# Differential attention: one ScalarE copy per head output, the sub-norm weight in a later product, and score matmuls of a unit under a scheduler priority

## Chip, cores and metric

The kernel runs on one core of one Trainium2 chip. The metric is device time in microseconds (us) of one execution; several executions are measured and the median is taken. One further execution was recorded by the hardware profiler; all rows of the profile come from it. TensorE is written PE in the profile (PEld is its weight load), VectorE DVE, ScalarE ACT, GpSimd POOL and SyncE SP.

## The reference, cut to what matters

Two layers work on 512 latent tokens and 256 context tokens of width 1024. Layer 0 is differential attention with 8 heads, layer 1 is grouped-query attention. The change lies in layer 0:

```python
def diff(qq, kk, vv, gate):
    o1 = sweep_attention(qq[..., 0, :], kk[..., 0, :], vv)
    o2 = sweep_attention(qq[..., 1, :], kk[..., 1, :], vv)
    o = o1 - lam.astype(o1.dtype) * o2
    o = rms_norm(o, subln_g) * (1.0 - lam_init)
    o = o.reshape(o.shape[0], o.shape[1], BRANCH_WIDTH)
    return (o * jax.nn.silu(gate)) @ w_out
```

Each head has two score maps of 64-wide queries and keys; their softmaxes are subtracted before the product with the values (128 wide). The head output `o` is normalised over its 128 features (`rms_norm`), weighted by `subln_g`, and gated.

## The kernel before

Every matrix product in float32 accuracy is made of three matmuls on a high part and a low part of each operand (`mm3`, lines 142 to 145; `pv_mm`, lines 147 to 150, for the product with the values). High parts are cast on ScalarE, low parts subtracted on DVE or POOL. PSUM is held in four single banks (`bk0` to `bk3`), handed out in turn by `pj` and `trp` and given back by `close`, and in two pairs of banks for scores (`sc0`, `sc1`, handed out by `sc2`).

A planner (`flow`, line 346) writes the program order of layer 0. For each head there are three streams: score units (S), transposes of the probabilities (T) and products with the values (M). Each step has a due time, a cost and lags to earlier steps; between steps the planner inserts pieces of the projections of later heads (`qk_proj`, `v_proj`, `z_proj`), which fill PE. A fourth stream (X) holds the sub-norm of each head (`subln`, line 974; `subln_last`, line 986, for the last head), a fifth the sums for the modulation weights (`grp_mm`, line 728).

The final order on each engine is made by the scheduler of the language. It takes instructions by priority: the place in the program less an offset that a step's `high_priority` gives, once their operands are ready by its own reckoning. The offsets of the streams in layer 0 are in `HOT0` (line 36): 4200 for S, 3100 for T, 0 for M and 4800 for X. Within an engine, instructions then run strictly in that order.

A score unit (`unit`, line 861) covers 128 queries against 768 keys. It issues 12 matmuls of 384 columns: two column halves, three high/low terms, and for each of these one matmul per map. The two maps use 64 rows each, rows 64 to 127 and rows 0 to 63 of the array. `after(prev)` (line 297) makes each come behind the one before it on PE; other matmuls may come between. `unit_ctx` (line 899) does the same for the 256 context queries with 12 matmuls of 256 columns. DVE takes the maximum (line 885), ScalarE the exponential (line 888), POOL and DVE scale and subtract the two maps (lines 893 and 896). PE transposes the result (line 945), ScalarE casts the high part `ah` (line 950), DVE subtracts the low part `al` (line 951), and `pv_mm` multiplies with the values.

A head output of 256 tokens stands in one bank when the last `pv_mm` of a chunk is done (`mstep`, line 954). There are 24 such outputs: 8 heads with 3 chunks. ScalarE squares it out of the bank into the tile `sq` (line 968), DVE multiplies it out of the bank by the sub-norm weight into `gT` (line 969 through the helper `scaled`, so that the profile shows line 221), and the bank is given back. The tile `sq` exists once. `subln` then takes the sum of squares over the 128 features by a matmul with ones (`colsum`, lines 377 to 382: a cast on ScalarE, a subtraction on POOL, two matmuls on PE), forms the inverse root by a logarithm and an exponential on ScalarE (lines 979 and 981), multiplies `gT` by it on DVE (line 982; line 997 for the last head) and by the gate on POOL (line 839).

Of the kernel before, what the change touches and what calls it, by code (L numbers as in the profile page):

```python
# [26 lines left out]
SC_A = 64 ** -0.5  # L27
SC_B = 128 ** -0.5
HOT = 500
HF0 = ((('qk', 1), ('qk', 2), ('z', 0)), (('qk', 3),), (('z', 1), ('v', 2), ('qk', 4), ('z', 2)), (('qk', 5), ('z', 3)), (('v', 4), ('qk', 6), ('z', 4)), (('qk', 7), ('z', 5)), (('v', 6), ('z', 6)), (('z', 7),))  # L30
FILL0 = tuple(f for hf in HF0 for f in hf)
ATT = 15.0
# [49 lines left out]
def tile_backbone(  # L82
# [134 lines left out]
    def scaled(eng, dst, src, s_):  # L217
        if eng == "a":
            nc.scalar.activation(dst, src, AF.Copy, scale=s_)
        else:  # L220
            (nc.vector if eng == "v" else nc.gpsimd).tensor_scalar(dst, src, s_, 1.0, ALU.mult, ALU.mult)  # L221
# [74 lines left out]

    def after(prev):
        return nullcontext() if prev is None else tc.issue_after(prev.ins)

    def hot(f, *args):  # L300
        with tc.high_priority(offset=HOT):
# [415 lines left out]
    with tc.tile_pool(name="t0", bufs=1) as t0:  # L717
# [140 lines left out]
        def s_units(h, qts):  # L858
            res = []

            def unit(qt):
                k0, nk = (0, T) if qt < NQ else (512, C)
                l, ps_ = small(2), []
                if nk == T:
                    sc = [sc2(), sc2()]
                else:
                    if h < KT - 1 or qt == NQ:
                        sts["sc"] = sc2()
                    sc = [sts["sc"]] * 2
                w = 384 if nk == T else 256  # L870
                qh, ql, kh_, kl_ = qk[h]
                tok = slice(qt * P, (qt + 1) * P)
                prev = None
                for j in range(nk // w):
                    c = slice(k0 + j * w, k0 + j * w + w)
                    for i, (a, b) in enumerate(((qh, kh_), (qh, kl_), (ql, kh_))):
                        for m in (1, 0):
                            r = slice(m * 64, m * 64 + 64)
                            with after(prev):
                                prev = nc.tensor.matmul(  # L880
                                    sc[m][:, j if nk == T else m, :w], a[r, tok], b[r, c], start=i == 0, stop=i == 2)
                for m in range(2):
                    scv = sc[m][:, :, :384] if nk == T else sc[m][:, m, :256]
                    mx = small()
                    nc.vector.tensor_reduce(mx, scv, AX.XY if nk == T else AX.X, ALU.max, negate=True)  # L885
                    pt = t0.tile([P, T], F32, tag=f"p{m}", name=nm("p"), bufs=4 if m == 0 else 2)[:, :nk]
                    pv_ = pt.rearrange("p (j n) -> p j n", j=2) if nk == T else pt
                    nc.scalar.activation(pv_, scv, AF.Exp, bias=mx, accum_out=l[:, m:m + 1])  # L888
                    ps_.append(pt)
                    r = l[:, m:m + 1]  # L890
                    nc.vector.reciprocal(r, r)
                    if m == 0:
                        scaled(EP0, pt, pt, r)
                    else:
                        nc.vector.tensor_tensor(r, r, nlam, ALU.mult)
                        nc.vector.scalar_tensor_tensor(ps_[0], pt, r, ps_[0], ALU.mult, ALU.add)  # L896
                        res.append(ps_[0])

            def unit_ctx():
                sc = [sc2(), sc2()]  # L900
                qh, ql, kh_, kl_ = qk[h]
                prev = None
                for qt in (NQ, NQ + 1):
                    tok = slice(qt * P, (qt + 1) * P)
                    for i, (a, b) in enumerate(((qh, kh_), (qh, kl_), (ql, kh_))):
                        for m in (1, 0):
                            r = slice(m * 64, m * 64 + 64)
                            with after(prev):
                                prev = nc.tensor.matmul(
                                    sc[m][:, qt - NQ, :C], a[r, tok], b[r, S:T], start=i == 0, stop=i == 2)  # L910
                l = [small(2), small(2)]
                pts = []
                for m in range(2):
                    mx = small(2)
                    nc.vector.tensor_reduce(mx, sc[m][:, :, :C], AX.X, ALU.max, negate=True)
                    pt = t0.tile([P, T], F32, tag=f"p{m}", name=nm("p"), bufs=4 if m == 0 else 2)
                    pts.append([pt[:, e * C:(e + 1) * C] for e in range(2)])
                    for e in range(2):
                        nc.scalar.activation(pts[m][e], sc[m][:, e, :C], AF.Exp, bias=mx[:, e:e + 1], accum_out=l[m][:, e:e + 1])
                    nc.vector.reciprocal(l[m], l[m])  # L920
                    if m:
                        nc.vector.tensor_tensor(l[m], l[m], nlam.to_broadcast([P, 2]), ALU.mult)
                    for e in range(2):
                        if m == 0:
                            scaled(EP0, pts[0][e], pts[0][e], l[0][:, e:e + 1])
                        else:
                            nc.vector.scalar_tensor_tensor(pts[0][e], pts[1][e], l[1][:, e:e + 1], pts[0][e], ALU.mult, ALU.add)
                res.extend(pts[0])

            if qts[0] == NQ and h < KT - 1:  # L930
                return res, [Step(unit_ctx, 1.0)]
            sts = {}
            cost = 1.2 if qts[0] < NQ else 0.5
            return res, [Step(lambda qt=qt: unit(qt), cost) for qt in qts]

        def pv_steps(h, at, ch, after, ts, ms):
            kts = range(6) if ch < 2 else range(4, 6)
            st = {}

            def tstep(kt):  # L940
                tr = trp()
                for e in range(2):
                    j = kt + e - kts[0]
                    for i, a in enumerate(at):
                        nc.tensor.transpose(tr[:, e * 256 + i * P:e * 256 + (i + 1) * P], a[:, j * P:(j + 1) * P], ident)  # L945
                if h == 0 and ch == 0 and kt == 0:
                    t0.tile([P, 8], F32, name="pad_a")
                ah = t0.tile([P, 512], F32R, tag="ah", name=nm("ah"), bufs=AB)
                al = t0.tile([P, 512], F32R, tag="al", name=nm("al"), bufs=AB)
                nc.scalar.copy(ah, tr)  # L950
                nc.vector.tensor_tensor(al, tr, f32(ah), ALU.subtract)
                st[kt] = ah, al

            def mstep(kt):
                if kt == kts[0]:
                    st["o"] = pj(256)
                o = st["o"]
                ah, al = st[kt]
                vh, vl = vt[h]
                vc = slice((h % 2) * P, (h % 2) * P + P)  # L960
                pv_mm(o, vh, vl, vc, ah, al, kt, kt == kts[0], kt == kts[-2])
                if kt == kts[-2]:
                    if ch == 2:
                        pvdone.add(h)
                    sl = slice(ch * 256, ch * 256 + 256)
                    if ch == 0:
                        ogs[h] = t0.tile([P, T], F32, tag="sq", name=nm("sq"), bufs=1)
                    nc.scalar.activation(ogs[h][:, sl], o, AF.Square)
                    scaled(EG0, gT[h][:, sl], o, subg)
                    close(o)  # L970

            chunk(0, tstep, mstep, kts[::2], [after], ts, ms)

        def subln(h):
            sq, og = ogs[h], gT[h]
            for (a, b) in halves:
                o2 = pj(384)
                colsum(o2, sq[:, a:b], [t0.tile([P, 512], F32R, tag="tmp", name=nm("sqs"), bufs=3)[:, :b - a] for _ in range(2)])
                nc.scalar.activation(sq[:, a:b], o2, AF.Ln, scale=1.0 / P, bias=eps)  # L979
                close(o2)  # L980
            nc.scalar.activation(sq, sq, AF.Exp, scale=-0.5)
            nc.vector.tensor_tensor(og, og, sq, ALU.mult)
            done.add((h, "o"))
            gate_mul(h)

        def subln_last(a, b):
# [7 lines left out]
            nc.scalar.activation(sq, o2, AF.Ln, scale=1.0 / P, bias=eps)  # L994
            close(o2)
            nc.scalar.activation(sq, sq, AF.Exp, scale=-0.5)
            nc.vector.tensor_tensor(og, og, sq, ALU.mult)
            VP[EGL].tensor_tensor(og, og, szt[h][:, a:b], ALU.mult)
            nc.scalar.copy(ghi[h][:, a:b], og)
            nc.vector.tensor_tensor(glo[h][:, a:b], og, f32(ghi[h][:, a:b]), ALU.subtract)  # L1000
# [692 lines left out]
```

## Time and profile before

| What | Value |
|---|---|
| runs | 824.39, 826.21 and 827.17 us; median 826.21 us |
| profiled execution | span 822.0 us from its first to its last instruction; no other time of it is given |
| granted TensorE clock, mean | 0.992 |
| DVE, ACT, POOL busy | 482.3, 457.1, 440.4 us |
| DMA | 77.77 MB, mean 95 GB/s |

The groups of the profile stand by line, engine, operation and tile: `L968 ACT ACTIVATE sq<-bk 128x256` is the square of line 968, read from a bank and written to `sq`. Behind it come the count, the busy time in us with the mean of one in ns, and the idle time of the engine just before such instructions with what ended it. In a row of the list of waits stand the waiting engine and line, what ended the wait, the sum in us, how often, and the longest. In a timeline row the first number is the start in us from the start of the span, the second the duration of the merged group. Ends of matmuls are modelled, so PE work is measured here from start to next start.

Layer 0's attention takes the span from about 81 us to 484 us, where the last head's sub-norm ends; layer 1's attention lies from about 620 us to 782 us.

### The profile page before, as it was taken

The page shows a single profiled execution, that of the slowest core. Times are in us where ns is not written, and L with a number is a line of the kernel's source. Part 1 is how long each engine was busy: PE and PEld are TensorE (multiplying, and loading weights), DVE is VectorE, ACT ScalarE, POOL GpSimd, SP SyncE. Part 2 cuts the span into 40 slices and gives each one's busy share as a digit, 9 for nine tenths or more (in the row PEclk, how much of TensorE's full clock was granted, in tenths as well). Part 3 has the DMA queues.
Part 4 walks back from the last instruction along what each step waited for, and adds up shares of the span by engine and source line. Part 5 has one row for each costly group of instructions (what it writes and reads, how often), then busy time and mean ns, then how long its engine had stood idle before and what let it go on. Part 6 is the DMA issues. An engine that isn't in the chain of part 4 may idle for free. (4 is left out here: it accounts for less than half of the span.)

```text
span 822.0 us, 14412 instructions
## 1 busy us (share of the span) xinstructions
PE 792.7 (96%) x5482; PEld 703.0 (86%) x5482; DVE 482.3 (59%) x896; ACT 457.1 (56%) x1001; POOL 440.4 (54%) x538
## 2 busy tenths in 40 slices
PE   7999999999999999999999999999999999999997
PEld 5678897788887898787988898889999899898986
DVE  3425566754768524675458952579546566755534
ACT  6534357664575544765556852674446576666631
POOL 4544766856367744665822311587788656733101
PEclk9999999999999999999999999999999999999999
DMA  9934211122053321323330045033421210301102
GB/s 300 347 131 142 77 39 52 52 77 90 28 154 98 122 101 65 116 78 118 113 104 26 27 151 182 1 110 103 154 79 52 78 52 1 103 26 52 50 28 103
DMA packets 41540, 77.77 MB, mean 95 GB/s; under 512 B 3584, under 2 KB 18688, under 8 KB 41472
## 3 DMA queue, kind: packets, MB, share of 16 engines
q1 hardware_dynamic: 38048, 71.71, 26.4%
q10 hardware_dynamic: 3424, 5.15, 1.8%
q8 instruction: 43, 0.70, 0.3%
q14 instruction: 25, 0.20, 0.1%
HBM read 70.56 MB, written 2.10 MB: 88 GB/s over the span
## 5 line engine op out<-in xcount | busy, mean ns | idle before, releaser
L207 POOL TENSOR_TENSOR wlo<-raw,whi 128x256 fp32r<-128x256 f32 x200 | 152.0, 792 | 72.8 <-ACT whi L213 63.1
L143 PE MATMUL bk<-whi,h 128*128 128x256 f32 (+1 forms) x592 | 176.9, 302 | 1.1 <-ACT p L1459 0.8
L144 PE MATMUL bk<-wlo,h 128*128 128x256 f32 (+1 forms) x592 | 176.2, 299 | 0.2 <-DVE wlo L207 0.2
L145 PE MATMUL bk<-whi,h 128*128 128x256 f32 (+1 forms) x592 | 175.4, 299 | 0.2 <-DVE h L1272 0.2
L143 PE MATMUL bk<-h,whi 128*128 128x512 f32 (+2 forms) x416 | 147.4, 354 | 2.7 <-ACT sq L979 1.5
L144 PE MATMUL bk<-h,whi 128*128 128x512 f32 (+2 forms) x416 | 144.8, 348 | 0.0
L145 PE MATMUL bk<-h,wlo 128*128 128x512 f32 (+2 forms) x416 | 144.8, 348 | 0.0
L143 PEld LDWEIGHTS bk<-whi,h 128*128 128x128 f32 x592 | 112.6, 191 | 8.2 <-issue 2.8
L145 PEld LDWEIGHTS bk<-whi,h 128*128 128x128 f32 x592 | 112.0, 190 | 4.7 <-issue 0.8
L144 PEld LDWEIGHTS bk<-wlo,h 128*128 128x128 f32 x592 | 112.3, 190 | 3.9 <-DVE wlo L207 0.4
L221 POOL TENSOR_SCALAR p<-p,sm 128x768 f32<-128x768 f32 (+1 forms) x80 | 67.1, 842 | 76.5 <-DVE sm L1460 28.7
L143 PEld LDWEIGHTS bk<-h,whi 128*128 128x128 f32 x416 | 78.2, 188 | 15.1 <-issue 4.0
L213 ACT CAST whi<-raw 128x1024 fp32r<-128x1024 f32 x64 | 67.1, 1048 | 36.1 <-PE bk L144 17.7
L145 PEld LDWEIGHTS bk<-h,wlo 128*128 128x128 f32 x416 | 78.3, 188 | 8.8 <-issue 1.6
L144 PEld LDWEIGHTS bk<-h,whi 128*128 128x128 f32 x416 | 78.4, 188 | 7.2 <-issue 0.8
L888 ACT ACTIVATE p<-sc,sm 128x768 f32<-128x768 f32 (+1 forms) x68 | 59.7, 881 | 37.9 <-DVE sm L885 37.9
L885 DVE TENSOR_REDUCE sm<-sc 128x1 f32<-128x768 f32 (+1 forms) x68 | 60.3, 917 | 17.4 <-PE sc L880 17.3
L181 POOL TENSOR_TENSOR sz<-sz,za 128x384 f32<-128x384 f32 (+1 forms) x24 | 28.1, 1172 | 42.8 <-ACT za L180 42.7
L896 DVE SCALAR_TENSOR_TENSOR p<-p,sm,p 128x768 f32<-128x768 f32 (+1 forms) x34 | 40.1, 1179 | 16.5 <-POOL p L221 14.9
L1480 DVE TENSOR_TENSOR al<-bk,ah 128x512 fp32r<-128x512 f32 x48 | 32.6, 687 | 26.1 <-ACT ah L1479 25.9
L950 ACT CAST ah<-bk 128x512 fp32r<-128x512 f32 x56 | 31.7, 590 | 27.9 <-PE bk L945 24.4
L880 PE MATMUL sc<-qk,qk 64*128 64x384 f32 (+1 forms) x396 | 45.8, 354 | 1.1 <-ACT p L888 1.0
(247 smaller groups left out, 1693.0 us busy)
## 6 DMA issues: line engine op xcount, KB each, us to landing
raw<-in_a_w SPq DMA_DIRECT2D x30, 512.0 KB, 3.6
araw<-in_ada_w SPq DMA_DIRECT2D x12, 1024.0 KB, 5.6
raw<-in_b_w SPq DMA_DIRECT2D x20, 512.0 KB, 3.5
ag<-in_ada_w SPq DMA_DIRECT2D x32, 256.0 KB, 6.9
raw<-in_w_out SPq DMA_DIRECT2D x16, 512.0 KB, 3.5
sw<-qr ACTq DMA_DIRECT2D x32, 128.0 KB, 2.5
gw<-in_ada_w SPq DMA_DIRECT2D x8, 512.0 KB, 3.8
xt<-in_x SPq DMA_DIRECT2D x4, 512.0 KB, 5.3
```

Of the source, the lines that this page charges most:

```text
L143: nc.tensor.matmul(o, ahi, bhi, start=start, stop=False)
L144: nc.tensor.matmul(o, ahi, blo, start=False, stop=False)
L145: nc.tensor.matmul(o, alo, bhi, start=False, stop=stop)
L207: eng.tensor_tensor(dst[:, i:i + n], a[:, i:i + n], b[:, i:i + n], op)
L213: nc.scalar.copy(hi, r)
L221: (nc.vector if eng == "v" else nc.gpsimd).tensor_scalar(dst, src, s_, 1.0, ALU.mult, ALU.mult)
L880: prev = nc.tensor.matmul(sc[m][:, j if nk == T else m, :w], a[r, tok], b[r, c], start=i == 0, stop=i == 2)
L885: nc.vector.tensor_reduce(mx, scv, AX.XY if nk == T else AX.X, ALU.max, negate=True)
L888: nc.scalar.activation(pv_, scv, AF.Exp, bias=mx, accum_out=l[:, m:m + 1])
L896: nc.vector.scalar_tensor_tensor(ps_[0], pt, r, ps_[0], ALU.mult, ALU.add)
L950: nc.scalar.copy(ah, tr)
L1480: nc.vector.tensor_tensor(al, tr, f32(ah), ALU.subtract)
```

## The change

In `mstep` ScalarE now copies the head output out of the bank into `gT` unscaled, the bank is given back, and ScalarE squares `gT`, now read from SBUF, into `sq`. The DVE multiplication by `subg` is gone there; the product in `subln` and `subln_last` takes the weight with it as a three-operand instruction. In `unit` and `unit_ctx` every matmul but the first gets a priority offset of 20000 on top.

```diff
+RUN = 20000
...
+    def chained(prev):
+        return nullcontext() if prev is None else tc.high_priority(offset=RUN)
...
-                            with after(prev):
+                            with after(prev), chained(prev):
                                 prev = nc.tensor.matmul(
                                     sc[m][:, j if nk == T else m, :w], a[r, tok], b[r, c], start=i == 0, stop=i == 2)
...
-                            with after(prev):
+                            with after(prev), chained(prev):
                                 prev = nc.tensor.matmul(
                                     sc[m][:, qt - NQ, :C], a[r, tok], b[r, S:T], start=i == 0, stop=i == 2)
...
                         ogs[h] = t0.tile([P, T], F32, tag="sq", name=nm("sq"), bufs=1)
-                    nc.scalar.activation(ogs[h][:, sl], o, AF.Square)
-                    scaled(EG0, gT[h][:, sl], o, subg)
+                    nc.scalar.copy(gT[h][:, sl], o)
                     close(o)
+                    nc.scalar.activation(ogs[h][:, sl], gT[h][:, sl], AF.Square)
...
-            nc.vector.tensor_tensor(og, og, sq, ALU.mult)
+            nc.vector.scalar_tensor_tensor(og, og, subg, sq, ALU.mult, ALU.mult)
             done.add((h, "o"))
...
-            nc.vector.tensor_tensor(og, og, sq, ALU.mult)
+            nc.vector.scalar_tensor_tensor(og, og, subg, sq, ALU.mult, ALU.mult)
             VP[EGL].tensor_tensor(og, og, szt[h][:, a:b], ALU.mult)
```

## Prediction, made before the changed kernel was run

> **What bounds the kernel now.** I read the page first, then the busy time of the stretch in which the change lies.
>
> ```profile
> span 822.0 us, 14412 instructions
> PE 792.7 (96%) x5482; PEld 703.0 (86%) x5482; DVE 482.3 (59%) x896; ACT 457.1 (56%) x1001; POOL 440.4 (54%) x538
> ```
> ```profile
> 112.00:490.00 378.00, 368.25 (x2627) 321.81 (x2626) 238.54 (x411) 226.24 (x480) 209.24 (x207) 1.00 0.25 82
> ```
>
> The second row is the window view from the first head output to the end of layer 0: length, then busy time and instructions of PE, PEld, DVE, ACT and POOL, then granted clock and DMA. PE is busy for 368.25 of 378 us; the other engines have at least 139 us to spare. So PE bounds this stretch. Two things can shorten it: fewer or shorter PE steps, or part of the 9.75 us in which PE is idle. The waits of PE from 80 to 492 us say what ends that idle time:
>
> ```profile
> PE bk L945 <- DVE al L951: 2.0, 2, 1.6
> ...
> PE bk L736 <- DVE al L951: 1.0, 1, 1.0
> PE bk L150 <- DVE al L951: 0.9, 2, 0.5
> ...
> PE bk L143 <- DVE gT L221: 0.7, 1, 0.7
> ...
> PE bk L736 <- DVE gT L221: 0.6, 1, 0.6
> ```
>
> The last two are waits for the instruction that the change removes, 1.3 us in all. The first three are the low part `al` of the transposed probabilities, 3.9 us, made by ScalarE and then DVE.
>
> **The change part by part.** First the head outputs. These are the groups that go, or that stand near to what comes:
>
> ```profile
> L968 ACT ACTIVATE sq<-bk 128x256 f32<-128x256 f32 x24 | 9.3, 385 | 8.8 <-PE bk L150 8.2 <-ACT ah L950 0.6
> ...
> L1493 ACT COPY g<-bk 128x256 f32<-128x256 f32 x16 | 6.1, 382 | 6.7 <-PE bk L150 6.7
> ...
> L1521 ACT CAST h<-g 128x256 fp32r<-128x256 f32 x2 | 0.8, 406 | 0.7 <-DVE g L1520 0.7
> ```
> ```profile
> L896 DVE SCALAR_TENSOR_TENSOR p<-p,sm,p 128x768 f32<-128x768 f32 x32 | 38.1, 1192 | 16.4 <-POOL p L221 14.9
> ...
> L221 DVE TENSOR_SCALAR gT<-bk,subg 128x256 f32<-128x256 f32 x24 | 11.5, 478 | 2.0 <-ACT sq L968 1.4
> L982 DVE TENSOR_TENSOR gT<-gT,sq 128x768 f32<-128x768 f32 x7 | 9.5, 1362 | 2.4 <-ACT sq L981 2.4
> ```
>
> The new copy out of a bank is layer 1's L1493, 382 ns, in place of the square's 385. The new square reads SBUF; its nearest row is the 256-column cast L1521, 406 ns. So ScalarE gains 24 x (382 + 406 - 385) = 9.7 us of work, and DVE loses 24 x 478 = 11.5 us. The three-operand product with the weight isn't in the trace for these tiles. The nearest row for it, L896 with the same size and kinds of operand, takes 1192 ns where the present product L982 takes 1362; both vary with what runs beside them. Its bounds are 7 x 170 = 1.2 us less and, if the weight cost a second product, 7 x 1362 = 9.5 us more; I take nothing, because L896 is the same instruction. None of these is on PE, and each of the two engines has 139 us or more to spare: the cover is PE's own projections, and what comes to the front if it fails is the second rival below.
>
> What does reach PE is when the bank comes free. The timeline at two places:
>
> ```profile
> 153.54 2.04 DVE L896 SCALAR_TENSOR_TENSOR p<-p,sm,p 128x768 f32<-128x768 f32 x1 [2.15 <-POOL p L221]
> ...
> 154.54 0.38 ACT L968 ACTIVATE sq<-bk 128x256 f32<-128x256 f32 x1
> ...
> 155.51 1.27 DVE L915 TENSOR_REDUCE sm<-sc 128x2 f32<-128x512 f32 x2
> ...
> 156.70 0.47 DVE L221 TENSOR_SCALAR gT<-bk,subg 128x256 f32<-128x256 f32 x1
> ...
> 157.23 0.39 PE L143 MATMUL bk<-h,whi 128*128 128x256 f32 x1 [0.71 <-DVE gT L221]
> ...
> 371.43 0.47 DVE L221 TENSOR_SCALAR gT<-bk,subg 128x256 f32<-128x256 f32 x1
> ...
> 371.95 0.64 PE L736 MATMUL bk<-araw,s 128*32 128x512 f32 x4 [0.59 <-DVE gT L221]
> ```
>
> At 154.92 the square is done, but DVE is busy with other work until 156.70, holds the bank to 157.17, and PE starts 0.06 us later. With the copy the bank would be free near 154.92, 2.25 us earlier, which is more than the 0.71 us that PE waited. So I count both waits as gone: 1.3 us. The bounds are nothing, if the next wait stands right behind, and 9.75 us, all of PE's idle time, if DVE's relief reached every wait.
>
> For the last head the copy stands ahead of the square in the chain to the output projection, 0.4 us more:
>
> ```profile
> 480.13 0.73 POOL L380 TENSOR_TENSOR sqs<-sq,sqs 128x256 fp32r<-128x256 f32 x1 [6.50 <-ACT sqs L379]
> ...
> 482.71 0.28 PE L381 MATMUL bk<-sqs,ones_r 128*128 128x256 f32 x1
> ```
>
> Its sum of squares is ready at 480.86 and PE takes it at 482.71. These 1.85 us, filled with output-projection matmuls, cover it; without them it would cost 0.4 us.
>
> Now the score matmuls. PE start times, a whole unit first, then three broken ones:
>
> ```profile
> 143.26 1.32 PE L880 MATMUL sc<-qk,qk 64*128 64x384 f32 x12
> 144.51 0.33 PE L945 MATMUL bk<-ident,p 128*128 128x128 f32 x1
> ```
> ```profile
> 175.61 0.34 PE L143 MATMUL bk<-h,whi 128*128 128x384 f32 x1
> 175.79 0.34 PE L144 MATMUL bk<-h,whi 128*128 128x384 f32 x1
> 176.06 0.62 PE L880 MATMUL sc<-qk,qk 64*128 64x384 f32 x4
> 176.61 0.44 PE L381 MATMUL bk<-sqs,ones_r 128*128 128x384 f32 x1
> 176.98 0.79 PE L880 MATMUL sc<-qk,qk 64*128 64x384 f32 x5
> 177.70 0.44 PE L382 MATMUL bk<-sqs,ones_r 128*128 128x384 f32 x1
> 178.07 0.61 PE L880 MATMUL sc<-qk,qk 64*128 64x384 f32 x3
> 178.61 0.44 PE L145 MATMUL bk<-h,wlo 128*128 128x384 f32 x1
> ```
> ```profile
> 340.09 0.96 PE L880 MATMUL sc<-qk,qk 64*128 64x384 f32 x7
> ...
> 342.06 0.66 PE L945 MATMUL bk<-ident,p 128*128 128x128 f32 x4
> ```
> ```profile
> 376.17 0.45 PE L880 MATMUL sc<-qk,qk 64*128 64x384 f32 x2
> ...
> 378.00 0.39 PE L144 MATMUL bk<-h,whi 128*128 128x256 f32 x1
> ```
>
> A whole unit takes 144.51 - 143.26 = 1.25 us, so 12 matmuls pass as six pairs; the ordinary step of a 384-column matmul of full height is 0.18 us (175.61 to 175.79). The unit at 176.06 holds two sum-of-squares matmuls of the sub-norm, whose stream has the higher offset; they cut two pairs apart. It takes 2.55 us, less 1.25 and 2 x 0.18: 0.94 lost. The unit at 340.09 (7 and 5, one such matmul between) takes 1.97, so 0.54 lost; that at 376.17 (2 and 10) 1.83, so 0.40. Together 1.9 us of PE time, which the new offset, above that stream's, should give back. The sum-of-squares matmul then waits for up to one unit, 1.25 us; behind it on PE nothing is held, and its Ln on ScalarE follows that much later. Bounds for the whole part: nothing, and 2.8 us if the three units that are cut after their first pair at the start of a head, by 0.3 us each as at 376.17 without the loss of its sum matmul, heal too. I leave these out, since there the next operand and not the priority may be what is late. Each whole unit already costs the same before and after.
>
> ```profile
> L143 PEld LDWEIGHTS bk<-h,whi 128*128 128x128 f32 x416 | 78.2, 188 | 15.1 <-issue 4.0
> ```
>
> [...]
>
> The sum against the profiled execution: 822.0 - 1.3 - 1.9 = 818.8 us of span. The median of the runs lies 4.2 us above that span, for what is outside it and for the spread of runs, and I carry it over: 823.0 us, 0.4% less.
>
> **The rivals.** *Nothing that can be told (0.22).* The pairs stay cut, because the scheduler finds the next operand late rather than the priority low; only the banks help, 826.2 - 1.3 = 824.9; or PE's freed time turns into the waits for `al`, up to 3.9 us of which stand next in the list, and 826 stays. For it: only 9.75 us of idle time was there to take. Against it: in the three cuts that I count it was the sub-norm's matmul that came between.
>
> *Slower through ScalarE (0.28).* Copy and square now come one behind the other on ScalarE, and the square's 406 ns stands ahead of the next cast `ah`, on which `al`, and so PE, waits. Each time this meets a waiting PE it costs 0.4 us; it decides from 8 of 24 on, where 8 x 0.4 = 3.2 eats the gain. At 16 of 24 the time is 826.2 - 3.2 + 6.5 = 829.5, at all 24 it is 832.7. For it: `al` is the longest wait, and the instruction order of all engines is made anew. Against it: ScalarE is idle for 152 of 378 us.
>
> *More than counted (0.10).* DVE's 11.5 us less work and the early banks take half of the other 8.45 us of PE's idle time: 823.0 - 4.2 = 818.8.
>
> **How the numbers follow.** The forecast has 0.40, with an own range of 821 to 825. A measurement of this kernel can tell about 0.3%, 2.5 us: faster is below 823.7, slower above 828.7. Of the forecast I put 0.32 below 823.7 and 0.08 above. Faster is 0.32 + 0.10 = 0.42, same 0.08 + 0.22 = 0.30, slower 0.28. The range goes from 818.5, just inside the third rival, to 831.0, between 16 and 24 meetings of the second, and leaves out what lies beyond on both sides.
>
> **What would show it.** Right: no row in which PE waits for `gT` or the head outputs' copy, 24 copies of about 0.38 us, DVE some 11 us less busy, and the sum-of-squares matmuls before or behind groups of 12 score matmuls, never inside. Wrong: PE waits for `al` growing beyond 3.9 us, squares of much over 0.41 us, new products of more than 1.4 us, or score groups of 2, 4, 5 or 7. If all steps are as said and the time still rises, the order elsewhere was made worse, and the waits of PE outside these rows would have grown.

## The result, and the profile after

| Kernel | Median, us | Lowest to highest | Runs |
|---|---|---|---|
| before | 825.27 | 823.88 to 827.81 | 11 |
| changed | 822.80 | 821.71 to 824.74 | 11 |

The ratio is 0.9971, with a 95% interval of 0.9962 to 0.9980: 2.5 us less, where the working had counted 3.2. The profiled execution of the changed kernel took 823.18 us at a span of 821.3, so 1.9 us lie outside its span, as in all its runs. In the 62 later executions of the kernel before it is 2.3 to 2.4 us. So some 0.45 us of the 2.5 lie outside the span, where the prediction counted nothing; no row of a profile shows why. By this measure the profiled execution of before, with its span of 822.0, took about 824.4 us (an estimate), 0.9 below the median of its runs, and that of the changed kernel 0.4 above its own. The two spans therefore set a quick execution beside an ordinary one; the medians carry the comparison, and the profiles only say where it comes from. The granted clock makes little of the difference: its mean is 0.994 over the 11 runs of the changed kernel and 0.993 over those 62.

From the page of the changed kernel:

```profile
span 821.3 us, 14395 instructions
PE 791.3 (96%) x5482; PEld 701.2 (85%) x5482; DVE 473.2 (58%) x872; ACT 464.6 (57%) x1025; POOL 437.4 (53%) x538
```

DVE is 9.1 us less busy and ScalarE 7.5 us more. The groups of the new instructions:

```profile
L974 ACT ACTIVATE sq<-gT 128x256 f32<-128x256 f32 x24 | 10.1, 424 | 0.3
L972 ACT COPY gT<-bk 128x256 f32<-128x256 f32 x24 | 9.0, 376 | 7.4 <-PE bk L151 7.3
...
L986 DVE SCALAR_TENSOR_TENSOR gT<-gT,subg,sq 128x768 f32<-128x768 f32 x7 | 9.0, 1286 | 0.2 <-ACT sq L985 0.2
```

The copy takes 376 ns (382 were taken for it), the square out of SBUF 424 (406), the product with the weight 1286 (it was taken to cost no more than the 1362 of the product before). The window view from 112 to 490 us has PE busy for 1.4 us more than before's 368.25, in the same 378 us, but with the same 2627 matmuls: a stretch of 3.4 us at a granted clock of 0.50 (last section) makes some of them longer. A second execution of the same program, `after_again`, gets 2647 done in this window.

```profile
112.00:490.00 378.00, 369.64 (x2627) 323.07 (x2626) 229.96 (x389) 233.63 (x505) 206.48 (x207) 1.00 0.25 82
```

The waits of PE from 80 to 492 us:

```profile
PE sc L884 <- ACT p L892: 2.0, 2, 1.0
PE bk L949 <- DVE p L900: 0.9, 1, 0.9
PE bk L145 <- DVE wlo L208: 0.8, 1, 0.8
PE bk L740 <- DVE al L955: 0.8, 1, 0.8
PE bk L949 <- DVE al L955: 0.6, 2, 0.4
...
PE bk L949 <- ACT gT L972: 0.5, 1, 0.5
...
PE bk L151 <- DVE al L955: 0.4, 1, 0.4
```

Both waits for DVE's `gT` (0.7 and 0.6 us) are gone; one wait of 0.5 us for the new copy has come in another place. The waits for `al`, which the slower rival had growing, fell from 3.9 to 1.8 us, and in `after_again` to 1.0. Something else went that the prediction had not taken up, a row of the kernel before in the same list:

```profile
PE bk L143 <- ACT sq L979: 1.5, 1, 1.5
```

At 451.57 us PE waits there for a bank with a sum of squares, until the logarithm of the sub-norm has read it. This wait stands in the kernel before and in all four variants below that leave the head outputs as they were; at this place no variant with the new head outputs has it (`dve_evac` has one of 1.0 us at 343 us). Why it goes is not shown, since the order around it is another.

The timeline of PE at the two units that had held sum-of-squares matmuls, and at a modulation group (`grp_mm`, line 740 here):

```profile
175.51 1.32 PE L884 MATMUL sc<-qk,qk 64*128 64x384 f32 x12
...
190.66 1.05 PE L740 MATMUL bk<-araw,s 128*32 128x512 f32 x2
...
192.54 1.06 PE L740 MATMUL bk<-araw,s 128*32 128x512 f32 x6
193.53 0.39 PE L146 MATMUL bk<-whi,h 128*128 128x256 f32 x1
...
340.13 1.32 PE L884 MATMUL sc<-qk,qk 64*128 64x384 f32 x12
341.38 0.45 PE L386 MATMUL bk<-sqs,ones_r 128*128 128x384 f32 x1
...
372.08 1.07 PE L740 MATMUL bk<-araw,s 128*32 128x512 f32 x8
```

The units are whole, and the sum-of-squares matmul comes behind them (341.38). But a modulation group, four 32-wide matmuls of the program with two records each, which use a quarter of the array's columns and pass together in 1.0 us as at 372.08, is cut here into 2 and 6 records. Each piece takes 1.0 us alone, as long as all eight. Before had one of its twelve groups cut; the changed kernel has two.

### The profile page after: what moved, and what is told of

Read it like the earlier page. It is cut to its first block, busy times and chain, and to the rows that moved or that the text cites. A ratio compares the mean times of both kernels' runs of the same rounds, so it can differ in the third digit from the quotient of the medians.

```text
span 821.3 us, 14395 instructions
## 1 busy us (share of the span) xinstructions
PE 791.3 (96%) x5482; PEld 701.2 (85%) x5482; DVE 473.2 (58%) x872; ACT 464.6 (57%) x1025; POOL 437.4 (53%) x538
## 5 line engine op out<-in xcount | busy, mean ns | idle before, releaser
L144 PEld LDWEIGHTS bk<-whi,h 128*128 128x128 f32 x592 | 111.3, 188 | 8.5 <-issue 2.5
L146 PEld LDWEIGHTS bk<-whi,h 128*128 128x128 f32 x592 | 110.8, 188 | 6.8 <-issue 1.7
L900 DVE SCALAR_TENSOR_TENSOR p<-p,sm,p 128x768 f32<-128x768 f32 (+1 forms) x34 | 42.5, 1251 | 14.0 <-POOL p L222 11.8
L1484 DVE TENSOR_TENSOR al<-bk,ah 128x512 fp32r<-128x512 f32 x48 | 32.6, 688 | 26.1 <-ACT ah L1483 25.9
L955 DVE TENSOR_TENSOR al<-bk,ah 128x512 fp32r<-128x512 f32 x56 | 37.6, 684 | 17.3 <-ACT ah L954 17.2
```

What stands on the lines that cost most here:

```text
L144: nc.tensor.matmul(o, ahi, bhi, start=start, stop=False)
L146: nc.tensor.matmul(o, alo, bhi, start=False, stop=stop)
```

## Experiments

The kernels ran in three sets, each beside the kernel before on one chip, and each ratio is to before's runs of its set: 825.19 us (26 runs) for `score_only`, `head_only`, `kl_first` and `dve_kept`, 824.69 (23) for `score_grp`, `grp_only`, `kl_grp` and `bank_late`, 825.25 (13) for the others.

### The two parts alone

`score_only` is before with the priority offset alone; `head_only` is before with the copy, the late square and the moved weight alone.

```diff
# score_only, in unit and unit_ctx
-                            with after(prev):
+                            with after(prev), chained(prev):
```

> The kernel before with the priority offset alone; head outputs leave PSUM as before. Theory (the two parts add as counted, 1.9 us for the score pairs and 1.3 us for the banks): 1.9 us below the kernel before, ratio 0.9977; score matmuls in 29 whole groups of 12 and three cut 2 and 10; PE still waits for gT of line 221, about 1.3 us. Rival (the gain is an accident of the order that the scheduler made anew, not these terms): no relation to 1.9 us, and the ratio can be 1.000 or above. [...]

> The kernel before with the head outputs' copy, the later square and the weight in the sub-norm's product; no priority offset. Theory (parts add): 1.3 us below the kernel before, ratio 0.9984; PE waits for gT gone, DVE some 9 us less busy, ScalarE some 8 us more; score groups still cut by the sum-of-squares matmuls. Rival (ScalarE's further work costs PE): at or above 1.000, with longer waits of PE for al. Rival (accident of order): any ratio, with PE waits elsewhere that make up the difference.

`head_only` took 824.10 us, ratio 0.9990 (0.9978 to 1.0003): 1.1 us less than before in the medians, near the 1.3 counted, though the interval reaches no change. Of the 1.1 us, 0.44 lie outside the span (1.91 us there, 2.35 before). Its profile does not show the counted waits turned into time: both waits for `gT` are gone, but PE is idle for 9.62 us from 112 to 490 us, against 9.75 before,

```profile
112.00:490.00 378.00, 368.38 (x2627) 321.92 (x2626) 227.36 (x387) 234.57 (x504) 210.48 (x208) 1.00 0.25 81
```

since other waits, from 80 to 492 us, have grown (the first row was 1.0 us) or come new:

```profile
PE bk L736 <- DVE al L951: 1.6, 1, 1.6
PE bk L736 <- ACT qr L767: 1.3, 1, 1.3
```

`score_only` took 827.16 us, ratio 1.0024 (1.0014 to 1.0034): 2.0 us slower, where 1.9 us were to be gained. Its units are whole as expected, but for the three at the start of a head. What it lost instead shows in its timeline of PE:

```profile
372.91 1.06 PE L740 MATMUL bk<-araw,s 128*32 128x512 f32 x6
373.90 0.45 PE L385 MATMUL bk<-sqs,ones_r 128*128 128x384 f32 x1
374.28 1.05 PE L740 MATMUL bk<-araw,s 128*32 128x512 f32 x2
375.25 0.44 PE L386 MATMUL bk<-sqs,ones_r 128*128 128x384 f32 x1
```

and in the same kernel's waits of PE from 352 to 420 us, where before has only the 0.6 us for `gT`:

```profile
PE bk L949 <- DVE p L931: 1.0, 1, 1.0
PE bk L144 <- DVE al L955: 0.7, 1, 0.7
```

The sum-of-squares matmul, kept out of a score unit, now stands inside a 32-wide group, whose second piece costs 374.28 to 375.25, 0.97 us. With the waits for `p` and `al` that is 2.7 us lost in this stretch, less 0.6 for the wait that is gone and 0.4 for the unit that before has cut at 376.17: 1.7 net. By the starts of the score matmuls, counted from the first, `score_only` was 0.66 us ahead of before at about 355 us and 0.94 us behind at the end of the attention, 1.6 us of change. Behind the attention the two profiles drift apart by another 1.1 us, in steps of 0.2 to 0.5 us up to 630 us, the largest at a wait for `al` in layer 1, which the edit does not touch.

The parts do not add: +2.0 and -1.1 alone, -2.5 together.

### Is the displaced cut the cause?

`score_grp` is `score_only` with the same offset on the 32-wide groups, so that nothing can cut those; `grp_only` is before with the offset on the groups alone.

```diff
# in grp_mm
-                with after(prev):
+                with after(prev), chained(prev):
```

> The kernel before with the priority offset on the score matmuls, as in the run score_only, and the same offset also on the second to fourth matmul of each 32-column group of the modulation sums (grp_mm). In score_only two of the twelve groups are cut, 6 and 2 records, where before one was. Theory (the sum-of-squares matmul, kept out of the score unit, cut the next group, and a cut group takes 0.97 us more): both groups whole, 1.9 us below score_only, about as the kernel before, ratio 1.000. Rival (score_only lost its time elsewhere, by waits for al and for p that the new order brought): at least 1.0022, little below score_only.

> The kernel before with the offset on the groups of the modulation sums alone, none on score units; few places of PE's order change. Theory (a cut group costs PE 0.97 us): the one cut group whole, 1.0 us below the kernel before, ratio 0.9988. Rival (what is freed on PE is taken back by the next wait): 1.000.

`score_grp` took 825.00 us, ratio 1.0006 (0.9997 to 1.0014), by the ratios 1.5 us less than `score_only`, and 2.2 less by the medians; 1.9 were expected. Its timeline at the same group:

```profile
371.51 1.06 PE L740 MATMUL bk<-araw,s 128*32 128x512 f32 x8
372.50 0.45 PE L385 MATMUL bk<-sqs,ones_r 128*128 128x384 f32 x1
372.79 0.33 PE L386 MATMUL bk<-sqs,ones_r 128*128 128x384 f32 x1
```

The group passes in 0.99 us and the sum matmul comes behind. This pair of kernels differs in few places of PE's order. The price of a cut group on PE, 0.97 us, is shown by the timelines; that it comes back in the time is supported by this pair, and not by `grp_only` below. But no unit is now cut by a sum-of-squares matmul and no group at all, 1.9 + 1.0 us of PE time less than before, and the time is that of before. The kernel's waits of PE from 80 to 492 us show part of the rest, a wait for `p` of line 931 that is not in before's list, and a wait for `gT` that is still there:

```profile
PE bk L949 <- DVE p L931: 1.0, 1, 1.0
...
PE bk L144 <- DVE gT L222: 0.7, 1, 0.7
```

`grp_only` took 824.58 us, ratio 0.9992 (0.9982 to 1.0003; 0.9988 was expected): inconclusive, since the interval holds both the expected gain and none.

### What in the head part does it?

The prediction said that DVE, busy with other work, is what holds the bank. Three variants of the changed kernel bear on that. `dve_kept` leaves DVE its 24 multiplications, but in SBUF, after the bank is free. `bank_late` lets the square read the bank too, so that ScalarE gives it back later. `dve_evac` lets DVE make the copy, so that the bank waits for DVE's queue again.

```diff
# dve_kept, behind the square; and the products as before
+                    nc.vector.tensor_scalar(gT[h][:, sl], gT[h][:, sl], subg, 1.0, ALU.mult, ALU.mult)
# bank_late
                     nc.scalar.copy(gT[h][:, sl], o)
+                    nc.scalar.activation(ogs[h][:, sl], o, AF.Square)
                     close(o)
-                    nc.scalar.activation(ogs[h][:, sl], gT[h][:, sl], AF.Square)
# dve_evac
-                    nc.scalar.copy(gT[h][:, sl], o)
+                    nc.vector.tensor_copy(gT[h][:, sl], o)
```

> The changed kernel, but with the weight multiplied on DVE as before, now from SBUF into SBUF in place after the copy, so that DVE keeps its 24 instructions while the bank comes free as early as in the changed kernel; the product in the sub-norm has two operands again. Theory (the bank's release is what counts, DVE has slack): the same as the changed kernel within 0.3 us, ratio near 0.997. Rival (DVE's relief is what counts): 1.3 us or more slower than the changed kernel, ratio 0.9985 or above, with more waits of PE for al.

> The changed kernel, but with the square read from PSUM as before, so that the bank is given back after copy and square, about 0.4 us later than in the changed kernel; both are on ScalarE and DVE still has none of it. Theory (what counted was DVE's place behind other work in its queue, 0.5 us on average and up to 1.9, not the 0.4 us): the same as the changed kernel within 0.6 us, ratio 0.997 to 0.9975. Rival (each 0.4 us of bank time counts): 1.3 us or more above the changed kernel, ratio 0.9985 or above.

> The changed kernel, but DVE instead of ScalarE copies the head output out of the bank, and the square reads the copy as in the changed kernel. The bank again waits for DVE's queue, though for one instruction and no longer for the square before it. Cuts of score units and of 32-column groups are as many as in the changed kernel or one fewer. Theory (the head part gains because the bank's release left DVE's queue, behind which it stood up to 1.9 us): PE waits for gT's copy on DVE again, 1 us above the changed kernel, ratio 0.9985. Rival (any single copy does it, since the bank no longer waits for two engines one behind the other): as the changed kernel, 0.997. Rival (order decides): any value, with waits that are not for gT.

| Kernel | Median, us | Ratio (interval) |
|---|---|---|
| dve_kept | 822.69 | 0.9965 (0.9952 to 0.9978) |
| bank_late | 820.84 | 0.9955 (0.9942 to 0.9968) |
| dve_evac | 822.63 | 0.9962 (0.9948 to 0.9976) |

`dve_kept` is as fast as the changed kernel. In its groups the multiplications stand at their old count, 605 ns each instead of 478:

```profile
L975 DVE TENSOR_SCALAR gT<-gT,subg 128x256 f32<-128x256 f32 x24 | 14.4, 605 | 2.1 <-ACT sq L974 1.8
```

So DVE's relief is worth nothing that can be told. `bank_late` holds each bank by a square of 401 ns longer, and is not slower:

```profile
L973 ACT ACTIVATE sq<-bk 128x256 f32<-128x256 f32 x24 | 9.6, 401 | 0.0
```

PE waits for that square once, by the waits from 80 to 492 us,

```profile
PE bk L949 <- ACT sq L973: 0.8, 1, 0.8
```

yet the kernel is faster than the changed one by 1.3 us by the ratios and 2.0 by the medians. `dve_evac`, which I expected to lose the gain, keeps it; of DVE's copy PE waits for 0.4 us in all, from 80 to 492 us:

```profile
PE bk L949 <- DVE gT L972: 0.4, 1, 0.4
```

My theory that DVE's queue is what matters failed its test here. What the kernel before has and none of these four has is a bank that goes through two engines in turn, where the second comes to it late. From the end of the last product (ends of matmuls are modelled) to the bank's release I measure a mean of 1.98 us before, 1.07 in the changed kernel, 1.26 in `bank_late` and 0.95 in `dve_evac`, over the heads' outputs. That this second engine is what cost is the reading that fits these kernels; it is not shown. By the records of PE, `dve_kept` differs from the changed kernel in some 30 stretches of the order, but `bank_late` in some 90 and `dve_evac` in some 120, so that the last two say that no clear loss appeared, and not what a later release is worth.

### The pairs that the prediction left out

Three units at the start of a head stayed cut into 2 and 10, 0.3 us each. The third matmul of a unit takes the low part of the keys, which is made last. `kl_first` is the changed kernel with that term first, so that the whole unit waits for it; `kl_grp` adds the offset on the groups.

```diff
# in unit and unit_ctx
-                    for i, (a, b) in enumerate(((qh, kh_), (qh, kl_), (ql, kh_))):
+                    for i, (a, b) in enumerate(((qh, kl_), (qh, kh_), (ql, kh_))):
```

> The changed kernel, with the order of the three high/low terms of a score unit turned: the term with the low part of k comes first, then high by high, then the low part of q. Theory (every cut of a unit costs PE 0.3 us or more and nothing else hangs on it): all 32 units whole, 0.9 us below the changed kernel, ratio to the kernel before near 0.996. Rival (a unit that waits for the last operand starts later, and the maximum, exponential and products behind it with it): the same as the changed kernel, 0.997, or slower, with PE waits for the low part.

> The changed kernel with the term with k's low part first in each score unit, as in the run kl_first, and the offset on the groups of the modulation sums. Theory (cuts cost what they show on PE): every unit and group whole, 1.0 us below kl_first, ratio to the kernel before near 0.9946. Rival (freed time is taken back): 0.9958 as kl_first.

`kl_first` took 821.78 us, ratio 0.9958 (0.9943 to 0.9973), 1.0 us below the changed kernel. Its timeline at the start of head 4 has the unit whole:

```profile
251.29 0.40 PE L144 MATMUL bk<-h,whi 128*128 128x512 f32 x1
251.62 1.34 PE L884 MATMUL sc<-qk,qk 64*128 64x384 f32 x12
252.88 0.66 PE L949 MATMUL bk<-ident,p 128*128 128x128 f32 x4
```

The offset had not been what these units lacked; their operand was late, as the prediction supposed: at the start of head 1 PE now waits 0.5 us for a low part (121.43 us, line 784). By the way one of the two cut groups became whole as well, so this gain of 1.0 us has 0.9 + 1.0 us of healed cuts behind it, and not the 0.9 alone that had been expected. `kl_grp` healed the last group and took 821.16 us, ratio 0.9967 (0.9955 to 0.9979); the expected 0.9946 was missed, and it is not told apart from `kl_first`.

### How much does a mere new order move?

`ctrl_c` has nothing of the change: one of the planner's lags for the stream M goes from 4.5 to 4.6 us.

```diff
-LM = (4.5, 4.5)
+LM = (4.6, 4.5)
```

> The kernel before with one planner number moved: the lag from a transpose to its product in layer 0 from 4.5 to 4.6 us. Nothing of the change is in it; 27 places of PE's order differ from the kernel before. Rival that is tested (a new order alone moves the time by as much as the counted terms): more than 1 us away from the kernel before on either side. Theory (the terms counted by cuts and bank waits make up the difference): two more score units cut and the one cut group whole, 0.3 us or less from the kernel before, ratio 0.9996 to 1.0004.

It took 832.83 us, ratio 1.0086 (1.0070 to 1.0102): 7.6 us slower, three times the whole effect of the change. Its waits of PE from 80 to 492 us, the two largest:

```profile
PE bk L945 <- DVE al L951: 4.2, 3, 2.1
PE bk L736 <- DVE al L951: 2.5, 2, 1.5
```

The waits for `al` come to 7.6 us where before has 3.9. None of its groups is cut, but three more of its units are than before, where two had been expected. Behind three waits of PE between 252 and 262 us, 4.3 us together, two stretches of 3.4 us have a granted clock of 0.50 in its profile:

```profile
262.10:265.50 3.40, 2.65 (x9) 2.07 (x8) 3.37 (x6) 1.54 (x4) 0.31 (x1) 0.50 0.00 0
265.50:268.90 3.40, 3.40 (x9) 2.63 (x9) 2.52 (x7) 1.69 (x4) 0.91 (x1) 0.50 0.00 0
```

So one small change of the order moved this kernel, by waits, cuts and clock together, by more than any of the steps costed here. It is one trial, and it says that a comparison of two kernels that differ in many places of the order can bear some us of chance.

### The best of it together, and the changed kernel once more

`late_kl_grp` is `bank_late` with the two other edits, low keys first and offset on the groups. `after_again` is the changed kernel unaltered, profiled once more.

> The run bank_late with the two edits that made all score units and all 32-column groups whole (k's low part first, the priority offset on the groups). Theory (cuts cost what they show on PE): two cut score units of 0.3 us and one cut group of 0.97 us are gone, 1.6 us below bank_late, ratio near 0.9935. Rival (the low time of bank_late was its order's accident, and a new order loses it): about the time of the run kl_grp, ratio 0.996 to 0.9965.

> The changed kernel once more, unaltered, for a second profile. In the first one a stretch of half clock of 3.4 us followed PE's idle time at 431 us. [...] Rival (the place belongs to the program's order): again half clock from 431 to 435 us.

`late_kl_grp` took 819.97 us, ratio 0.9931 (0.9917 to 0.9945), 5.3 us less than before by the medians and 2.8 below the changed kernel: the best version, near the 0.9935 that was expected. All its units and groups are whole. The rival, that the low time of `bank_late` was an accident which a new order loses, did not come true. `after_again` took 820.70 us, span 818.8, against 823.18 and 821.3 for the same program in the first profile. The stretch of half clock at 431 us is missing, so the rival, that the place belongs to the program's order, did not come true; the section on the hardware shows it.

The cuts, counted in each profile at 0.97 us for a group, 0.3 for a unit at a head's start and the measured loss for a unit in the middle (head_only: 0.94 us in two units), beside the ratios:

| Kernel | Groups cut | Starts cut | PE time lost to cuts, us | Ratio |
|---|---|---|---|---|
| before | 1 | 3 | 3.8 | 1 |
| grp_only | 0 | 3 | 2.8 | 0.9992 |
| score_only | 2 | 3 | 2.8 | 1.0024 |
| score_grp | 0 | 3 | 0.9 | 1.0006 |
| head_only | 2 | 3 | 3.8 | 0.9990 |
| changed | 2 | 3 | 2.8 | 0.9971 |
| dve_kept | 2 | 3 | 2.8 | 0.9965 |
| dve_evac | 2 | 2 | 2.5 | 0.9962 |
| bank_late | 1 | 2 | 1.6 | 0.9955 |
| kl_first | 1 | 0 | 1.0 | 0.9958 |
| kl_grp | 0 | 0 | 0 | 0.9967 |
| late_kl_grp | 0 | 0 | 0 | 0.9931 |

In the lower eight, which have the head part, less lost time mostly goes with a lower ratio; in the upper four it does not. That fits a PE whose saved time is taken back by waits as long as its banks come free late. It is a pattern in twelve kernels, with the order's chance in each, and not shown by one pair. Cuts are not all, either: `kl_grp` and `late_kl_grp` have none, and their intervals lie apart. And healed cuts come back in part only. In the seven neighbouring pairs that differ only in priority or term order, and in which no cut is added, 10.1 us of cuts were healed and the medians, each against before of its set, fell by 5.2 us together: from 1.7 for 1.9 (`score_only` to `score_grp`) to a loss of 0.4 for 1.9 (`grp_only` to `score_grp`).

## Why the prediction was right, and where its steps were not

The measured 822.80 us lie 0.2 us from the forecast of 823.0, and that closeness is luck: the kernel before came out 0.9 us lower than the three runs that the prediction started from (825.27 against 826.21), and the gain 0.7 us smaller than counted.

- **The bound.** Right: PE, 369.64 of 378 us in the stretch. No other engine came to the front in the changed kernel.
- **Head outputs, 1.3 us.** The size came out near, 1.1 alone (its interval reaches nothing), and both waits for `gT` are gone. But 0.44 us of it lie outside the span, and PE's idle time in the stretch hardly changed (9.62 for 9.75 us), so the step that makes time of these two waits is not shown. It has a gap, too: the wait of 1.5 us for the sub-norm's logarithm, longer than both, went as well and was not counted. New, and not predicted, is a wait of 0.5 us for the copy itself. The reason was given too narrowly: "DVE is busy with other work until 156.70, holds the bank to 157.17" describes its place well, but in `dve_evac` the copy through DVE's queue, and in `bank_late` another 0.4 us in the bank, cost nothing that shows.
- **Costs laid to nothing.** Right as far as the rows go: no wait of PE for the new squares or the 1286 ns product stands in the list, and `dve_kept` shows that DVE's lighter load was not needed either. DVE lost 9.1 us, less than the 11 named as a sign. The 0.4 us on the last head's chain were not measured by themselves.
- **Score matmuls, 1.9 us.** Here a step failed, though the sum came out near: "The sum-of-squares matmul then waits for up to one unit, 1.25 us; behind it on PE nothing is held". Nothing is held behind it, but it goes somewhere: into the next open place, and in `score_only` that place was the middle of a 32-wide group, 0.97 us. With the waits for `p` and `al` the term changed its sign, +2.0 us alone. On top of the head part it was worth 1.3 us (824.10 to 822.80): in `head_only`'s order only two units were cut, by 0.94 us together, so there was less to heal than the trace of before had shown. The cuts had to be counted in the order that the other edit makes, which the trace of before does not show. Groups of 2 still stand at three starts of a head: the prediction had left these out of its sum, and yet listed groups of 2 as a sign of being wrong.
- **Cut and whole units.** That whole units save PE time is shown: the unit at 340 us takes 1.25 us whole in the changed kernel (340.13 to 341.38), where before took 1.97, of which 0.18 was the sum-of-squares matmul, so 0.54 less; in `head_only` the two cut units take 0.55 (274.10 to 276.08) and 0.39 us (341.35 to 343.17) more than 1.25 and 0.18. The row of weight loads in the prediction bears on the 0.18: line 143 has 416 loads there, 188 ns each in the mean, and a step of 0.18 us from one matmul to the next (175.61 to 175.79), so that the load was not paid on top of the matmul. The 822.80 by itself could not decide whether the saved time comes back, since the whole units alone made the kernel slower (827.16).
- **Span to median, 4.2 us.** As a distance it held two things: some 2.4 us outside the span of before, and some 1.8 us by which the median of the first three runs lay above the profiled execution. Neither carried over as it was: the changed kernel has 1.9 us outside its span, and the median of before fell by 0.9 us with more runs.
- **The rivals.** Slower through ScalarE: the waits for `al`, its sign, went down by 2.1 us, so it did not happen. More than counted: `bank_late` and its like come to 818.8's neighbourhood (819.97 for the best), but with edits that healed cuts and made the order anew; DVE's relief was worth nothing that can be told in `dve_kept`. No change that can be told: the point that PE's freed time turns into waits is what `score_only`, `score_grp` and in its profile `head_only` did, so this rival describes each part alone.
- **What stays open.** Why the two parts together gain more than their sum. Why `bank_late` is faster than the changed kernel: 1.3 us fewer of cuts (one group, one start) would nearly do, but with no cuts left on either side `late_kl_grp` is still faster than `kl_grp`, and the same edit made the order anew. And why `kl_grp` did not gain over `kl_first`.

## What to carry to other kernels

Where a scheduler fills an engine by priority, keeping one group of matmuls together pushes what used to cut it into the next open place: look at where it lands, and protect that place in the same edit. Before trusting a gain of a few us on such a kernel, change one constant of the order that should do little (here 0.1 us of lag moved 7.6 us), and test a single price with two kernels whose orders differ in few places. Try giving a PSUM bank one reader, or two on the same engine: the variants here fit the view that which engine it is matters less than that no second queue stands between, though none shows it by itself.

## What the runs showed of the hardware

**Cut column groups.** The eight records of a 32-column group pass in 1.0 us together, and pieces of 2 and 6 take 1.0 us each (0.98 for 2 at 190.66 us, 0.99 for 6 at 192.54; the pieces of 4 and 4 at 244.55 us take 0.98): the price of a piece did not depend on how many records it has, up to eight.

**Half clock in the middle of work.** The window view of the changed kernel's first profile, with the granted clock third from the end:

```profile
428.50:431.90 3.40, 2.49 (x21) 2.16 (x21) 3.23 (x9) 2.77 (x8) 1.00 (x2) 1.00 0.00 0
431.90:435.30 3.40, 3.40 (x18) 3.18 (x17) 2.54 (x5) 1.74 (x4) 0.90 (x1) 0.50 0.00 0
```

and of the same program in `after_again`:

```profile
428.50:431.90 3.40, 2.51 (x21) 2.19 (x21) 2.61 (x10) 3.40 (x9) 1.90 (x2) 1.00 0.00 0
431.90:435.30 3.40, 3.40 (x29) 3.02 (x28) 3.29 (x6) 0.75 (x3) 0.00 (x0) 1.00 0.00 0
```

PE was busy for 2.49 (73%) and 2.51 us of the 3.4 us before, and in one execution the next 3.4 us ran at half clock (0.50), 18 matmuls instead of 29, in the other not (1.00). In the timeline of the first,

```profile
432.62 0.63 PE L151 MATMUL bk<-ah,vlo 128*128 128x256 f32 x2
433.05 0.63 PE L151 MATMUL bk<-al,vhi 128*128 128x256 f32 x2
```

a pair of steps takes 0.43 us from start to start, and in the timeline of `after_again` 0.23:

```profile
431.29 0.40 PE L151 MATMUL bk<-ah,vlo 128*128 128x256 f32 x2
431.52 0.40 PE L151 MATMUL bk<-al,vhi 128*128 128x256 f32 x2
```

By the starts of the score matmuls this stretch cost 1.3 to 1.5 of the 2.5 us between the two executions. By windows of 0.2 us the clock of the first falls within 431.80 to 432.00 us (0.81) and is back within 435.20 to 435.40 (0.65). The kernel before, at the same place, was busy for less, 1.83 us, and kept a clock of 1.00, here and from 431.90 to 435.30 us:

```profile
428.50:431.90 3.40, 1.83 (x18) 1.75 (x17) 3.40 (x9) 2.87 (x7) 0.99 (x1) 1.00 0.00 0
```

`grp_only` was busy for more than that, 2.22 us, and had 0.50 in the 3.4 us behind:

```profile
426.30:429.70 3.40, 2.22 (x22) 1.88 (x18) 2.67 (x5) 2.74 (x7) 0.99 (x1) 0.99 0.02 5
429.70:433.10 3.40, 3.01 (x14) 3.01 (x15) 3.20 (x11) 1.68 (x5) 0.91 (x1) 0.50 0.00 0
```

In both of these kernels PE waits there once for `al`, 1.6 us (from 426 to 434 us). So in these four profiles neither the program nor PE's idle time just before tells whether the clock falls; what sets it off is not shown. One profile of a kernel can be off by as much as the effect of this change: the two executions of the changed kernel lie 2.5 us apart.
